# The low parts of the up-projection's weights: a subtraction on VectorE, or a negated copy and a DMA that adds

## The chip, the cores and the metric

The kernel runs on one core of one Trainium2 chip. The metric is the device time of one execution in microseconds. The profiled execution and the three timed runs are executions of the same program. PE is TensorE, DVE is VectorE, ACT is ScalarE, POOL is GpSimd, SP is the engine that only issues DMAs here.

## The reference

One decoder layer over 1024 tokens of width 1024, in float32. The part that the change touches is the gated MLP:

```python
def conv_ffn(xn, w_up, conv_w, conv_b, w_down):      # w_up: 1024 x 5632
    u = xn @ w_up
    upad = jnp.pad(u, ((0, 0), (CONV_WIDTH - 1, 0), (0, 0)))
    c = conv_b
    for j in range(CONV_WIDTH):
        c = c + upad[:, j:j + S] * conv_w[j]
    gate, val = jnp.split(c, 2, axis=-1)
    return (jax.nn.silu(gate) * val) @ w_down
```

Ahead of it stand an RMSNorm, two attention branches, their merge and a mixing projection; behind it a last RMSNorm.

## The kernel before, in words

Every float32 matrix product is made of three products of a reduced type, fp32r: an operand is split into a high part (a cast on ACT) and a low part (operand minus high part, on DVE), and PE adds high by high, high by low and low by high into one PSUM bank. The stages follow each other: input projection (`project`), attention, branch merge (`rest`), mixing projection (`mix`), up-projection (`hidden`), down-projection (`down`).

The change lies in `hidden`, which the profile shows from about 680 us to about 1100 us. The weights come as 22 pairs of 128 columns, one for the gate (`g`) and one for the value (`v`). A pair and the two halves of the tokens make a 2x2 block product, done with seven products in place of eight. The weight operands of the seven are `A11` and `A12` (the two halves of `g`), four sums `S1` to `S4`, and `A22` (half of `v`). So for each pair:

- SP loads `g` into a `raw` tile (three buffers) and `v` into an `rv` tile (two buffers).
- POOL makes the sums: `sa` (S1, S2) and `sb` (S3, S4), two instructions of 128x512 each, into `sf` tiles (two buffers: one for `sa`, one for `sb`, each used again by the next pair).
- `split_pair` splits four tiles: `g` into `wh`, `wl`; `sa` into `sh`, `sl`; `sb` into `sh`, `sl` (three buffers of each for both); half of `v` into another `wh`, `wl` (one buffer). These are the lines L127 (cast on ACT) and L128 (subtraction on DVE).
- PE multiplies in the order P1 (A11), P2 (A12), P5 (S1), P6 (S2), P7 (S3), P3 (S4), P4 (A22), 12 matmuls each, 84 for a pair.
- DVE and one ACT copy put the seven results together into two `us` tiles (`recombine`, L461 to L470); POOL multiplies each by the norm's factors (L1083); ACT and DVE do the convolution, the silu and the gating in `glu_halves` (L1089 to L1094); SP stores the result to `hd`.

The weights of pair j+1 are taken, and those of pair j+2 begun, while PE works on pair j. Each engine runs its own queue in order, and an instruction that waits holds back all behind it on its engine. A scheduler sets the order in the queues when the program is built; `issue_after` and `high_priority` steer it. A tile's buffer is written again only when all that read it are done. Below, pair A is the one that PE works on, B the next, and "C" the one after B.

Of the kernel before, what the change touches and what calls it, by code (L numbers as in the profile page):

```python
# [10 lines left out]
F32 = mybir.dt.float32  # L11
F32R = mybir.dt.float32r
AF = mybir.ActivationFunctionType
ALU = mybir.AluOpType
# [10 lines left out]
NF = DFF // P  # L25
# [19 lines left out]
class Trunk:  # L45
    def __init__(self, tc, ins, out):
        self.tc, self.nc = tc, tc.nc
        (self.xT, self.w_in, self.w_br, self.w_mix, self.w_up, self.w_dn,
         self.vecs_d, self.bias_d) = ins
        self.out = out  # L50
        self.uid = 0
        self.stores = []
        self.uw = self.w22 = self.behind = None
        self.pin, self.after = False, None
        self.hs, self.defer, self.late = {}, [], []

    def name(self, s):
# [12 lines left out]
    def ahead(self, n):  # L70
        while len(self.wq) < n and self.wsrc and (self.wsrc[0][1] != "pair" or self.uw):
            src, nk, *eng = self.wsrc.pop(0)
            if nk == "sums":

                self.sums = self.split_pair(*self.sum_pair(src, True, "sl"), 1, 3)
            elif nk == "rest":
                self.sums["A22"] = self.load_w(src[1][:, 4:8], 4)
                self.wq.append(self.sums)
            elif nk == "second":
                self.wq.append(self.second_pair(src, *eng))  # L80
            elif nk == "idle":
                self.wq.append(self.load_w(src, 8, None, (self.uw, "sh", "sl")))
            elif nk == "pair":
                first, skip = eng or (False, 0)
                self.wq.append(self.split_pair(*self.sum_pair(src, first), skip))
            else:
                self.wq.append(self.load_w(src, nk, *eng))
        if self.deep and self.wsrc and len(self.wsrc[0]) == 2 and not isinstance(self.wsrc[0][1], str):

            src, nk = self.wsrc[0]  # L90
            self.wsrc[0] = src, nk, None, None, self.load_raw(src, nk)
# [20 lines left out]
    def split_pair(self, g, v, sa, sb, skip=0, end=4):  # L112

        nc = self.nc
        ops = {}
        for pool, h, l, src, names in ((self.wp, "wh", "wl", g, ("A11", "A12")), (self.uw, "sh", "sl", sa, ("S1", "S2")),
                                       (self.uw, "sh", "sl", sb, ("S3", "S4")), (self.w22 or self.wp, "wh", "wl", v[:, 1:2], ("A22",)))[skip:end]:
            n = len(names)
            hi = self.tl(pool, [P, n, 4, P], h, F32R)
            lo = self.tl(pool, [P, n, 4, P], l, F32R)  # L120
            with ExitStack() as queue:
                if self.pin and ops:
                    for i in done:
                        queue.enter_context(self.tc.issue_after(i.ins))
                if self.after is not None and names[0] == "A11":
                    queue.enter_context(self.tc.issue_after(self.after.ins))
                i = nc.scalar.copy(hi, src)  # L127
                j = nc.vector.tensor_tensor(lo, src, hi.bitcast(F32), ALU.subtract)  # L128
            if not ops:
                done = i, j  # L130
            if names[0] in ("A11", "A22"):
                ops["made", names[0]] = i, j
            for i, name in enumerate(names):
                ops[name] = hi[:, i], lo[:, i]
        self.pin, self.after = False, None
        return ops
# [1310 lines left out]
```

## Time and profile before

| | us |
|---|---|
| median of 3 runs | 1343.81 (1343.46 to 1343.99) |
| the profiled execution | 1342.57 |
| its span, first to last instruction | 1340.4 |
| PE busy in the span | 1319.8 (98%) |
| DVE busy | 1068.0 (80%) |
| ACT busy | 621.2 (46%) |
| POOL busy | 497.0 (37%) |
| subtractions on L128, all stages | 87.6 + 76.6 + 49.3 in three groups |

The granted TensorE clock of the core is 0.997. POOL issues no DMA at all in this kernel: the queues with dynamic DMAs are those of SP and ACT. The busy share of an engine is an average over stages with different limits, so the stage of the up-projection is read by itself below, in stretches and in single instructions in order of time.

### The profile page before, as it was taken

To read this page: it belongs to the slowest core of one execution; us is meant where nothing else is said; L and a number is where in the kernel's file an instruction comes from. 1 tells how busy PE (TensorE), PEld (TensorE's weight loads), DVE (VectorE), ACT (ScalarE), POOL (GpSimd) and SP (SyncE) were. 2 spreads that over 40 slices of the span, in tenths; PEclk is the share of its full clock that TensorE was granted. 3 is DMA by queue.
4 is the path that set the end of the run, shared out by engine and by line. 5 is a ranking of instruction groups with operands and counts; after the bars stand their busy time and mean duration, and the time that the engine had idled before them with its cause. 6 is when DMAs were issued, how large, how long until landed. Compare 5 with 4: busy or idle time off the path is not lost.

```text
span 1340.4 us, 17301 instructions
## 1 busy us (share of the span) xinstructions
PE 1319.8 (98%) x6264; PEld 1096.7 (82%) x6264; DVE 1068.0 (80%) x1605; ACT 621.2 (46%) x1019; POOL 497.0 (37%) x365
## 2 busy tenths in 40 slices
PE   7999999999999999999999999999999999999997
PEld 6888888888888778878888888888888888888787
DVE  8847775289889876565678999999999997979975
ACT  8432232276667665333454444444444444323544
POOL 0436552000102124651446555655556510224412
PEclk9999999999999999999999999999999999999999
DMA  6423343876553235334423122222222239672333
GB/s 258 151 103 150 147 157 141 247 181 189 142 139 132 91 120 196 141 111 157 133 104 110 64 95 79 94 79 79 95 79 90 75 97 336 203 259 63 114 123 126
DMA packets 63045, 182.64 MB, mean 136 GB/s; under 512 B 6896, under 2 KB 15216, under 8 KB 62960
## 3 DMA queue, kind: packets, MB, share of 16 engines
q1 hardware_dynamic: 51504, 164.13, 37.3%
q10 hardware_dynamic: 11456, 17.41, 3.6%
q8 instruction: 49, 0.80, 0.2%
q14 instruction: 36, 0.29, 0.1%
HBM read 130.66 MB, written 50.86 MB: 135 GB/s over the span
## 4 chain that ended last, share of the span: by engine, by line
PE 87%; DVE 4%; POOL 4%; DMA 2%; ACT 1%; issue 1%; POOLq 0%; SPq 0%; ACTq 0%; DVEq 0%
PE t L922 13%; PE t L920 13%; PE t L921 13%; PE g L209 3%; PE t L914 3%; PE g L210 3%; PE g L211 3%; PE sc L636 3%; PE y L1159 2%; PE d L1159 2%; PE sc L211 2%; PE d L921 2%; PE d L920 2%; PE sc L209 2%; PE sc L210 2%; PE d L922 2%
## 5 line engine op out<-in xcount | busy, mean ns | idle before, releaser
L1089 ACT ACTIVATE c<-us,vecs 128x512 f32<-128x512 f32 x80 | 61.3, 781 | 133.2 <-POOL us L1083 129.2
L1091 DVE SCALAR_TENSOR_TENSOR c<-us,vecs,c 128x512 f32<-128x512 f32 x160 | 110.5, 748 | 8.6 <-ACT c L1089 8.5
L1083 POOL TENSOR_TENSOR us<-us,rstd 128x1024 f32<-128x1024 f32 x38 | 99.7, 2642 | 4.5 <-DVE us L469 2.5
L128 DVE TENSOR_TENSOR sl<-sf,sh 128x1024 fp32r<-128x1024 f32 x62 | 87.6, 1415 | 11.5 <-ACT sh L127 11.5
L127 ACT CAST sh<-sf 128x1024 fp32r<-128x1024 f32 x62 | 63.4, 1048 | 60.3 <-PE t L921 43.9
L176 DVE TENSOR_TENSOR wl<-raw,wh 128x1024 fp32r<-128x1024 f32 (+2 forms) x46 | 57.7, 1256 | 31.4 <-ACT wh L174 20.0
L128 DVE TENSOR_TENSOR wl<-raw,wh 128x1024 fp32r<-128x1024 f32 (+1 forms) x35 | 76.6, 2187 | 3.7 <-ACT wh L127 3.6
L103 POOL TENSOR_TENSOR sf<-rv 128x512 f32<-128x512 f32 x30 | 41.2, 1375 | 100.9 <-DVE sl L128 57.9
L174 ACT CAST wh<-raw 128x1024 fp32r<-128x1024 f32 (+2 forms) x46 | 46.0, 1001 | 62.6 <-PE sc L210 30.5
L209 PE MATMUL g<-xh,wh 128*128 128x512 f32 x176 | 70.6, 401 | 0.1
L211 PE MATMUL g<-xh,wl 128*128 128x512 f32 x176 | 70.4, 400 | 0.0
L210 PE MATMUL g<-xl,wh 128*128 128x512 f32 x176 | 70.3, 399 | 0.0
L108 POOL TENSOR_TENSOR sf<-raw,rv 128x512 f32<-128x512 f32 x30 | 40.7, 1357 | 65.4 <-DVE sl L128 65.4
L619 POOL MEMSET aT<- 128x128 f32 x32 | 6.1, 204 | 151.6 <-PE t L665 101.3
L640 DVE CUSTOM_DVE_ANT_0 L<-sc,bias 128x128 f32<-128x128 f32 (+7 forms) x64 | 47.7, 752 | 17.0 <-PE sc L636 13.7
L641 ACT ACTIVATE L<-L,sm 128x128 f32<-128x128 f32 (+7 forms) x64 | 49.6, 779 | 20.0 <-DVE sm L640 17.4
L794 POOL TENSOR_TENSOR gr<-gr,rstd 128x1024 f32<-128x1024 f32 x16 | 39.9, 2500 | 41.6 <-DMA gr<-gd 41.5
L128 DVE TENSOR_TENSOR wl<-rv,wh 128x512 fp32r<-128x512 f32 x30 | 49.3, 1644 | 3.5 <-ACT wh L127 3.5
L1093 ACT ACTIVATE c<-c 128x512 f32<-128x512 f32 x40 | 23.9, 598 | 60.7 <-DVE c L1091 60.7
L636 PE MATMUL sc<-u,u 128*128 128x512 f32 (+2 forms) x192 | 49.7, 358 | 0.0
L211 PE MATMUL sc<-mh,wl 128*128 128x512 f32 x126 | 49.1, 390 | 0.4 <-DVE wl L176 0.4
L229 POOL TENSOR_TENSOR rs<-ms,mhalf 128x8 f32<-128x8 f32 (+2 forms) x9 | 13.6, 1516 | 95.7 <-DVE ms L227 85.1
(527 smaller groups left out, 4432.7 us busy)
## 6 DMA issues: line engine op xcount, KB each, us to landing
u<-qd SPq DMA_DIRECT2D x72, 256.0 KB, 6.4
raw<-in_w_in SPq DMA_DIRECT2D x25, 512.0 KB, 4.2
raw<-in_w_up SPq DMA_DIRECT2D x23, 512.0 KB, 3.5
hr<-hd SPq DMA_DIRECT2D x46, 256.0 KB, 5.3
hd<-c SPq DMA_DIRECT2D x22, 512.0 KB, 2.6
rv<-in_w_up SPq DMA_DIRECT2D x21, 512.0 KB, 3.5
raw<-in_w_down SPq DMA_DIRECT2D x19, 512.0 KB, 4.3
gr<-gd SPq DMA_DIRECT2D x16, 512.0 KB, 3.6
```

What stands on the lines that cost most here:

```text
L127: i = nc.scalar.copy(hi, src)
L128: j = nc.vector.tensor_tensor(lo, src, hi.bitcast(F32), ALU.subtract)
L209: nc.tensor.matmul(ps, wh[:, kc + o, :], ah, start=first and n == 0, stop=False)
L210: nc.tensor.matmul(ps, wh[:, kc + o, :], al, start=False, stop=False)
L211: nc.tensor.matmul(ps, wl[:, kc + o, :], ah, start=False, stop=last and n == len(kcs) - 1)
L636: nc.tensor.matmul(sc[:, lo + n0:lo + n1], qs, k[c][part][:, n0:n1], start=part == 0, stop=part == 1)
L920: nc.tensor.matmul(ps, ah[:, k, :], bh, start=first and n == 0, stop=False, skip_group_check=skip)
L921: nc.tensor.matmul(ps, ah[:, k, :], bl, start=False, stop=False, skip_group_check=skip)
L922: i = nc.tensor.matmul(ps, al[:, k, :], bh, start=False, stop=last and n == len(ks) - 1, skip_group_check=skip)
L1083: (nc.vector if j == 0 else nc.gpsimd).tensor_tensor(u[:, 2:], u[:, 2:], self.rstd, ALU.mult)
L1089: nc.scalar.activation(c, u[:, o + 2:o + 2 + H2], AF.Identity, bias=self.vecs[:, C_CB + m:C_CB + m + 1], scale=col(m, 2))
L1091: nc.vector.scalar_tensor_tensor(c, u[:, o + k:o + k + H2], col(m, k), c, ALU.mult, ALU.add)
```

## The change

From the third pair of the up-projection on, the low part is made in another way. ACT writes the negated high part into the low tile (one more ACT instruction for each split), and POOL issues a DMA that adds the raw operand, read from SBUF, onto it. The flag `by_dma` is set when a pair is begun and counts pairs (nine pairs belong to the input projection; the first pair of the up-projection is begun elsewhere and isn't counted). It is true for the third to the last pair of the up-projection, and it is still true when the first sums of the down-projection are split (`"sums"`, two tiles). In all there are 82 such DMAs: 62 of 128x1024 (512 KB each) and 20 of 128x512 (256 KB each). The high parts, the products and their order on PE stay.

```diff
         self.pin, self.after = False, None
+        self.by_dma, self.npairs = False, 0
...
                 first, skip = eng or (False, 0)
+                self.npairs += 1
+                self.by_dma = len(self.pairs) + 1 < self.npairs < len(self.pairs) + NF
                 self.wq.append(self.split_pair(*self.sum_pair(src, first), skip))
...
                 i = nc.scalar.copy(hi, src)
-                j = nc.vector.tensor_tensor(lo, src, hi.bitcast(F32), ALU.subtract)
+                if self.by_dma:
+                    j = nc.scalar.mul(lo, hi.bitcast(F32), -1.0)
+                    nc.gpsimd.dma_start(lo, src, accum_op=ALU.add)
+                else:
+                    j = nc.vector.tensor_tensor(lo, src, hi.bitcast(F32), ALU.subtract)
```

In the program the changed lines stand seven lines further down (L127 is L130, L103 is L106, L1083 is L1090). A semaphore named DMASW counts DMAs that POOL issued, DMAHW those of SP and ACT.

POOL's queue before, one pair in the middle of the stage (`us` 7265 and 7266 are the results of the pair before the one on PE, `sf` 7436 and 7437 are `sa` and `sb` of a pair to come):

```order
L1083 TENSOR_TENSOR us_7265<-us_7265,rstd 128x1024 [waits DVE_49]
L1083 TENSOR_TENSOR us_7266<-us_7266,rstd 128x1024 [waits DVE_49]
L103 TENSOR_TENSOR sf_7436<-rv_7434 128x512 [waits DMAHW2_49,Activation_49,Pool_49]
L107 TENSOR_TENSOR sf_7436<-sf_7436,raw_7432 128x512 [waits DMAHW5_49,Pool_49]
L1082 MEMSET us_7421 128x2 [waits DVE_49,Activation_49]
L108 TENSOR_TENSOR sf_7437<-raw_7432,rv_7434 128x512 [waits DVE_49]
L109 TENSOR_TENSOR sf_7437<-raw_7432,sf_7436 128x512 [waits Pool_49]
```

POOL's queue now, one pair in the middle of the stage. `sl_7318` is the low part of S3, S4 of pair A (read by P7), `wl_7323` that of A22 of pair A (read by P4), `sf_7461` is `sb` of pair B, `sl_7472` the low part of S1, S2 of B, `us` 7444 and 7445 are the results of the pair ahead of A, and `sf_7619`, `rv_7617`, `wl_7626` and `raw_7615` belong to pair C:

```order
L133 DMA sl_7318<-sf_7302 128x1024 [waits Activation_49]
L1089 MEMSET us_7603 128x2 [waits DVE_49]
L111 TENSOR_TENSOR sf_7461<-raw_7456,rv_7458 128x512 [waits DMASW7_49]
L112 TENSOR_TENSOR sf_7461<-raw_7456,sf_7460 128x512 [waits Pool_49]
L1090 TENSOR_TENSOR us_7444<-us_7444,rstd 128x1024 [waits DVE_49]
L133 DMA sl_7472<-sf_7460 128x1024 [waits Activation_49]
L1090 TENSOR_TENSOR us_7445<-us_7445,rstd 128x1024 [waits DVE_49]
L133 DMA wl_7323<-rv_7299 128x512 [waits DMASW5_49,Activation_49]
L106 TENSOR_TENSOR sf_7619<-rv_7617 128x512 [waits DMAHW6_49,DMASW0_49,Pool_49]
L1089 MEMSET us_7604 128x2 [waits DVE_49,Activation_49,Pool_49]
L133 DMA wl_7626<-raw_7615 128x1024 [waits DMAHW7_49,DMASW2_49,Activation_49]
L110 TENSOR_TENSOR sf_7619<-sf_7619,raw_7615 128x512 [waits Pool_49]
```

Behind these twelve rows the next `sl` DMA begins the same sequence for the next pair. Four DMA issues stand between POOL's eight instructions of a pair, and where the sums waited for DVE they wait for POOL's own DMAs (DMASW7 is the DMA that wrote `sl_7318`, DMASW0 the one that wrote `sl_7472`).

SP's queue before, in the middle of the stage (`rv` is the load of a `v`, `hd` the store of a result):

```order
L98 DMA raw_7742<-in_w_up 128x1024 [waits DMAHW3_49,DVE_49,Pool_49]
L1095 DMA hd<-c_7307 128x1024 [waits DVE_49]
L100 DMA rv_7589<-in_w_up 128x1024 [waits DMAHW7_49,DMAHW5_49,DVE_49]
L98 DMA raw_7897<-in_w_up 128x1024 [waits DMAHW6_49,DVE_49,Pool_49]
L1095 DMA hd<-c_7462 128x1024 [waits DVE_49]
```

SP's queue now, with the load of `rv_7617` for pair C:

```order
L101 DMA raw_7774<-in_w_up 128x1024 [waits DMASW2_49,Activation_49,Pool_49]
L103 DMA rv_7458<-in_w_up 128x1024 [waits DMAHW3_49,DMAHW5_49,DMASW5_49,Activation_49]
L1102 DMA hd<-c_7331 128x1024 [waits DMAHW4_49,DVE_49]
L101 DMA raw_7933<-in_w_up 128x1024 [waits DMASW6_49,Activation_49,Pool_49]
L103 DMA rv_7617<-in_w_up 128x1024 [waits DMAHW0_49,DMAHW6_49,DMASW1_49,Activation_49]
```

The order of the three kinds of DMA is the same; the loads of `raw` and `rv` wait for POOL's DMAs (DMASW1 is the one that wrote `wl_7323`) where they waited for DVE.

## The prediction

> **What bounds the kernel now.** I read the page's busy times first, then stretches of the up-projection by themselves, then single instructions of each engine in order of time. The page:
>
> ```profile
> span 1340.4 us, 17301 instructions
> PE 1319.8 (98%) x6264; PEld 1096.7 (82%) x6264; DVE 1068.0 (80%) x1605; ACT 621.2 (46%) x1019; POOL 497.0 (37%) x365
> ```
>
> PE is idle for 1340.4 - 1319.8 = 20.6 us in the whole span, and that is all that any relief of another engine could give back. Where it lies shows in the busy times by stretch (length, then PE, PEld, DVE, ACT, POOL, granted clock, DMA share, GB/s):
>
> ```profile
> 740.00:1050.00 310.00, 310.00 (x1370) 256.68 (x1369) 301.09 (x352) 133.45 (x182) 173.90 (x133) 1.00 0.25 83
> 1090.00:1190.00 100.00, 100.00 (x442) 82.80 (x442) 80.79 (x105) 39.69 (x58) 15.60 (x11) 1.00 0.68 229
> 1190.00:1340.00 150.00, 140.44 (x677) 117.59 (x675) 118.63 (x161) 61.39 (x96) 49.98 (x32) 0.97 0.37 130
> ```
>
> In the steady part of the up-projection PE is busy 310.00 of 310.00 us. DVE is at 301.09 of 310 (97%), but PE never waits for it. So the stage is PE's, and its length is the number of pairs by the time of 84 matmuls. PE's own timeline gives that time, the first matmul of pairs 3, 9, 10 and 22 (j = 2, 8, 9 and 21 in the code):
>
> ```profile
> 723.09 0.39 PE L914 MATMUL t<-B_0h,wh 128*128 128x512 f32 x1
> ...
> 837.33 0.39 PE L914 MATMUL t<-B_0h,wh 128*128 128x512 f32 x1
> 856.37 0.39 PE L914 MATMUL t<-B_0h,wh 128*128 128x512 f32 x1
> ...
> 1084.85 0.39 PE L914 MATMUL t<-B_0h,wh 128*128 128x512 f32 x1
> ```
>
> The period T is 856.37 - 837.33 = 19.04 us, and (1084.85 - 723.09) / 19 = 19.04 as well: no pair is late. A product takes 19.04 / 7 = 2.72 us, so with s the start of a pair P7 starts at s + 10.9 and P4 at s + 16.3; its first use of a low part is the third matmul, so A22's low part is due at s + 16.8.
>
> What the other engines do in a pair is in the groups of the stretch 740 to 1050 (busy us, mean ns | idle before, what ended it):
>
> ```profile
> L1083 POOL TENSOR_TENSOR us<-us,rstd 128x1024 f32<-128x1024 f32 x33 | 88.0, 2685 | 4.4 <-DVE us L469 2.5
> L128 DVE TENSOR_TENSOR wl<-raw,wh 128x1024 fp32r<-128x1024 f32 x16 | 47.7, 2981 | 0.0
> L128 DVE TENSOR_TENSOR sl<-sf,sh 128x1024 fp32r<-128x1024 f32 x34 | 43.2, 1269 | 0.0
> L127 ACT CAST sh<-sf 128x1024 fp32r<-128x1024 f32 x33 | 33.0, 1046 | 0.1
> L128 DVE TENSOR_TENSOR wl<-rv,wh 128x512 fp32r<-128x512 f32 x17 | 31.0, 1822 | 0.0
> L108 POOL TENSOR_TENSOR sf<-raw,rv 128x512 f32<-128x512 f32 x17 | 22.0, 1295 | 53.0 <-DVE sl L128 53.0
> L103 POOL TENSOR_TENSOR sf<-rv 128x512 f32<-128x512 f32 x16 | 20.7, 1293 | 29.3 <-DMA rv<-in_w_up 28.0 <-DVE sl L128 1.3
> L127 ACT CAST wh<-rv 128x512 fp32r<-128x512 f32 x17 | 10.6, 621 | 7.0 <-PE t L921 7.0
> ```
>
> POOL already waits twice in each pair for a buffer that the splits hold: about 53.0 / 17 = 3.1 us until DVE has read `sb`, and 28.0 / 16 = 1.8 us until the next `v` has been loaded. Both waits lie in the chain that the change lengthens.
>
> **What is removed.** For each of 20 pairs DVE loses 2.98 + 2 x 1.27 + 1.82 = 7.3 us, and two more subtractions of 1.27 us in the down-projection's first sums: about 149 us. PE waited for none of it in this stage, so it is worth nothing directly. It does free POOL: the group above has 2.69 us for a multiplication by `rstd`, but the spread within it is wide.
>
> ```profile
> L1083 POOL TENSOR_TENSOR us<-us,rstd x38: 1992/2448/2982, 733.8 to 1070.0; 128x1024 f32<-128x1024 f32 x38
> L128 DVE TENSOR_TENSOR wl<-raw,wh x35: 686/2432/3024, 59.1 to 1217.8; 128x1024 fp32r<-128x1024 f32 x31, 128x512 fp32r<-128x512 f32 x4
> ```
>
> (least, median, longest ns.) With DVE's subtractions gone I take the least, 1.99 us; with the mean the sum below would have 1.4 us more a pair. The Trainium skill (SBUF — State Buffer, Who interferes with whom) says that a DVE instruction with both inputs in SBUF contends with a GpSimd instruction that reads SBUF. By that rule the 1.99 us should be reached, since no such DVE instruction is left in a pair; without it the total below would be some 25 us higher.
>
> **What is added on ACT and the DMA engines.** The negations are 62 of 128x1024 and 20 of 128x512. At the casts' price that is 62 x 1.046 + 20 x 0.621 = 77 us, 3.8 us a pair. ACT goes from 133.45 / 310 x 19.04 = 8.2 us to 12.0 us of 19.04: covered. The DMAs write 3 x 512 + 256 KB = 1.84 MB a pair, 96 GB/s beside the 83 GB/s at which the engines are 0.25 busy; even counted twice that leaves room. Nothing queued on SP behind the load of `rv` is wanted earlier: it is the store of a result that ACT and DVE finish after that.
>
> **What is added on POOL, the term that decides.** POOL now issues four DMAs a pair, and two instructions wait for one of these to land. I follow POOL's queue as shown above from the `sl` DMA of S3, S4 of one pair to that of the next:
>
> 1. the `sl` DMA is issued and must land (call it X512), as the next `sb` overwrites what it reads;
> 2. two sums, 2 x 1.29;
> 3. the first `rstd` multiplication, 1.99; a DMA issue (q); the second, 1.99;
> 4. the `wl` DMA of A22 is issued and must land (X256), since it reads the `rv` buffer that pair C's `v` is to be loaded into;
> 5. SP loads that `v`, and POOL makes the first sum from it;
> 6. a sum 1.29, a DMA issue (q), a sum 1.29; then step 1 again.
>
> Step 5 is seen in the timelines of DVE, SP and POOL today, where DVE's subtraction stands in the place of the DMA:
>
> ```profile
> 862.23 1.89 DVE L128 TENSOR_TENSOR wl<-rv,wh 128x512 fp32r<-128x512 f32 x1
> 864.15 0.33 SPq L100 DMA_DIRECT2D rv<-in_w_up  x1
> 867.74 1.29 POOL L103 TENSOR_TENSOR sf<-rv 128x512 f32<-128x512 f32 x1 [1.76 <-DMA rv<-in_w_up]
> ```
>
> From the buffer's release (862.23 + 1.89 = 864.12) to POOL's sum it is 3.6 us. So a turn takes C = 2.58 + 3.98 + 3.6 + 2.58 + 2q + X512 + X256 = 12.74 + 2q + X512 + X256. No row has a DMA issued by POOL, nor one that adds, so q and X are bounded by the nearest rows: DMA issues (KB each, median us to landing), and the smallest arithmetic on POOL.
>
> ```profile
> u<-qd SPq DMA_DIRECT2D x72, 256.0 KB, 6.4
> hd<-c SPq DMA_DIRECT2D x22, 512.0 KB, 2.6
> rv<-in_w_up SPq DMA_DIRECT2D x21, 512.0 KB, 3.5
> xr<-in_xT SPq DMA_DIRECT2D x7, 512.0 KB, 7.2
> gd<-u ACTq DMA_DIRECT2D x2, 256.0 KB, 2.8
> out_T<-x ACTq DMA_DIRECT2D x2, 256.0 KB, 2.1
> L229 POOL TENSOR_TENSOR rs<-ms,mhalf 128x8 f32<-128x8 f32 (+2 forms) x9 | 13.6, 1516 | 95.7 <-DVE ms L227 85.1
> ```
>
> For q: not under SP's 0.33 us, hardly over the 1.5 us of POOL's smallest operation; I take 0.9, the middle. For the landing: the two transfers of this very stage take 2.6 and 3.5 us for 512 KB, mean 3.05; 256 KB take 2.1 to 2.8, mean 2.45. An addition moves three streams (two read, one written) where a copy moves two, so I take 1.5 times: X512 = 0.9 + 4.6 = 5.5 and X256 = 0.9 + 3.7 = 4.6. Then C = 12.74 + 1.8 + 10.1 = 24.6 us, 5.6 us over T. Low ends: q 0.33 and copies of 2.6 and 2.1 us issue included, C = 18.1. High ends: q 1.5, 7.2 and 6.4, C = 29.3.
>
> **The sum.** Pair 3 (s = 723.09) is the first. A22's one buffer is free when P4 of pair 2 has ended, 723.5; cast and negation bring 724.7. One X256 and one turn later A22 of pair 4 has landed: 724.7 + 4.6 + 24.6 = 753.9. It is due at 723.09 + 19.04 + 16.8 = 758.9, so 5.0 us are in hand. 18 turns follow up to pair 22, each 5.6 us longer than PE's: 18 x 5.6 - 5.0 = 96 us. The two DMAs in the down-projection are far from use. The profiled execution had 1342.57 us, so 1439; from the median of 1343.81, about **1440 us**.
>
> **The rivals.** I count 0.2% (2.7 us) as what a measurement can tell from no change.
>
> *Hidden* (0.10): the turn fits under PE's. That needs 18 (C - 19.04) to stay below 758.9 - 724.7 - X256 - C, which with X256 = 3 means C under 19.7. At the low ends C is 18.1 and PE waits nowhere: 1344 us, not slower. For it: POOL is busy only 173.90 of 310 us in the stage, and `hd<-c` does leave SBUF in 2.6 us. Against it: q would have to be near SP's 0.33 us and the addition as quick as the quickest copy.
>
> *Cheap additions* (0.20): an addition costs a copy's time behind the issue, X512 = 0.9 + 2.6 and X256 = 0.9 + 2.1. C = 12.74 + 1.8 + 6.5 = 21.0; 18 x 2.0 less 10.2 in hand (34.2 - 3.0 - 21.0) is 26 us, so 1370. For it: most of these 2 to 3 us doesn't grow with the size (2.1 for 256 KB, 2.6 for 512), so a third stream may cost little. The Trainium skill (DMA: Bandwidth & Descriptors, Anatomy of one DMA — SWDGE (gpsimd) path) has about 2.0 us plus bytes over 436 GB/s for a DMA on this path, and about 1 us to its first byte. An estimate from that page is 3.2 and 2.6 us with q = 1, so C = 20.5 and 1360 us; no run here shows yet that it holds for a DMA that adds.
>
> *Dear additions* (0.18): the adding itself is slow, or POOL is held for longer than 1.5 us by an issue. At the high ends C = 29.3; 18 x 10.3 + 1.6 is 187 us, so 1531, and more if an addition takes over 7 us. For it: DMAs of 256 KB do take 6.4 us where the queues are full, and POOL's small operations show a start cost of 1.5 us. Against it: the DMA engines are a quarter busy in this stage.
>
> *Faster* (0.02): PE's 20.6 us of idling would have to shrink, and almost none of it lies behind the stage's splits (9.6 us are in the last 150 us).
>
> **How the numbers follow.** The forecast, C from 22.3 to 27.5, has 0.50; it spans 1395 to 1495. The range 1362 to 1545 leaves out the hidden case, the cheapest additions and the dearest, about 2 in 10. Faster 0.02, the same 0.10, slower 0.88.
>
> **What would show it.** Right: in the steady stretch PE idles some 5 to 6 us a pair ahead of P4's first low matmul, released by the `wl<-rv` DMA; POOL idles ahead of the `sb` sum (on the `sl` DMA, about 4.6 us) and ahead of the first sum (on `rv`, about 8 us); pair starts are 24 to 25 us apart; the landings are 5.5 and 4.6 us; `rstd` multiplications take 2.0 us. Wrong: PE stays at 310 of 310 (hidden); pair starts under 22 us apart (cheap); PE released by ACT or DVE, or DMA engines busy throughout (another bound); POOL issues that each hold it for several us.

## The result and the profile after

The changed kernel takes 1431.43 us (median of 6 runs, 1427.77 to 1434.04); the kernel before took 1342.67 us in the same comparison (6 runs). The ratio is 1.066 [1.0647, 1.0673], so the change costs 6.6%. The profiled execution has a span of 1432.0 us, 91.6 us more than before.

The page of the kernel after, its span and the busy times:

```profile
span 1432.0 us, 17503 instructions
PE 1358.6 (95%) x6264; PEld 1111.6 (78%) x6264; DVE 936.9 (65%) x1523; ACT 696.9 (49%) x1101; POOL 541.1 (38%) x447
```

DVE loses 131 us and POOL, for all its new work, is busy 38% of the time. No engine's share betrays a bound. The same stretch of the up-projection as before, by engines (length, then PE, PEld, DVE, ACT, POOL, granted clock, DMA share, GB/s):

```profile
740.00:1050.00 310.00, 276.44 (x1112) 217.71 (x1112) 152.91 (x226) 156.34 (x201) 164.11 (x157) 0.94 0.60 147
```

PE, which had no idle time here, has 33.6 us of it, and it does less in the stretch: 1112 recorded matmuls where there were 1370. The pair starts in PE's timeline (j = 4, 10 and 21):

```profile
768.74 0.40 PE L921 MATMUL t<-B_0h,wh 128*128 128x512 f32 x1
...
908.39 0.39 PE L921 MATMUL t<-B_0h,wh 128*128 128x512 f32 x1
...
1168.38 0.39 PE L921 MATMUL t<-B_0h,wh 128*128 128x512 f32 x1
```

The mean period is (1168.38 - 768.74) / 17 = 23.5 us, 4.5 over T; single pairs take 20.1 to 26.8 us. Pair 22 starts 83.5 us later than before (1168.38 against 1084.85), so all but 8 us of the 91.6 lie ahead of that start, in this loop. Of the 8, 4.9 are one wait of PE ahead of the down-projection's first matmul, for DVE's last result of pair 22 (`d L1166 <- DVE us L477`). POOL's timeline shows one turn of the loop, with SP's load in its place:

```profile
886.81 1.19 POOL L133 DMA_DIRECT2D sl<-sf  x1
...
893.79 1.29 POOL L111 TENSOR_TENSOR sf<-raw,rv 128x512 f32<-128x512 f32 x1 [5.67 <-DMA sl<-sf]
895.04 1.29 POOL L112 TENSOR_TENSOR sf<-raw,sf 128x512 f32<-128x512 f32 x1
896.28 1.99 POOL L1090 TENSOR_TENSOR us<-us,rstd 128x1024 f32<-128x1024 f32 x1
898.22 0.87 POOL L133 DMA_DIRECT2D sl<-sf  x1
898.84 2.29 POOL L1090 TENSOR_TENSOR us<-us,rstd 128x1024 f32<-128x1024 f32 x1
900.79 1.21 POOL L133 DMA_DIRECT2D wl<-rv  x1
907.94 1.29 POOL L106 TENSOR_TENSOR sf<-rv 128x512 f32<-128x512 f32 x1 [5.95 <-ACT c L1100]
...
909.23 0.87 POOL L133 DMA_DIRECT2D wl<-raw  x1
909.83 1.58 POOL L110 TENSOR_TENSOR sf<-sf,raw 128x512 f32<-128x512 f32 x1
911.07 1.18 POOL L133 DMA_DIRECT2D sl<-sf  x1
```

```profile
904.43 0.33 SPq L103 DMA_DIRECT2D rv<-in_w_up  x1
```

This is the turn that the prediction followed row by row: 911.07 - 886.81 = 24.3 us here, one of the longer ones (from 793 us on they take 23.2 to 24.8). POOL stands still twice, ahead of the `sb` sum until the `sl` DMA has landed, and ahead of the first sum until A22's DMA has landed and `v` has been loaded. The bracket at 907.94 names `ACT c L1100`, but that instruction is no input of the sum; SP's load, issued 3.5 us earlier, is. POOL's waits from 760 to 1160 us (us in total, times, longest) and the landings (KB, median us from issue):

```profile
POOL sf L111 <- DMA sl<-sf: 84.1, 17, 6.2
POOL sf L106 <- ACT c L1100: 78.4, 13, 6.1
POOL sf L106 <- DMA rv<-in_w_up: 18.4, 4, 6.0
```

```profile
sl<-sf POOLq DMA_DIRECT2D x40, 512.0 KB, 5.1
wl<-raw POOLq DMA_DIRECT2D x20, 512.0 KB, 5.2
wl<-rv POOLq DMA_DIRECT2D x20, 256.0 KB, 3.5
```

PE's timeline around P4 shows what it waits for:

```profile
902.51 0.50 PE L927 MATMUL t<-T_0h,wh 128*128 128x512 f32 x1 [1.97 <-ACT s L468]
...
904.41 0.51 PE L929 MATMUL t<-T_0h,wl 128*128 128x512 f32 x1 [1.16 <-DMA wl<-rv]
904.74 0.60 PE L927 MATMUL t<-T_1h,wh 128*128 128x512 f32 x1
905.15 0.63 PE L928 MATMUL t<-T_1l,wh 128*128 128x512 f32 x1
```

It waits 1.16 us for A22's low part, at the place that was forecast, but 1.97 us just before that for an ACT copy that frees a PSUM bank. ACT's timeline says why that copy is late:

```profile
898.31 0.78 ACT L1096 ACTIVATE c<-us,vecs 128x512 f32<-128x512 f32 x1 [7.81 <-POOL us L1090]
901.16 0.78 ACT L1096 ACTIVATE c<-us,vecs 128x512 f32<-128x512 f32 x1 [2.07 <-POOL us L1090]
901.88 0.58 ACT L468 COPY s<-t 128x512 f32<-128x512 f32 x1
```

It stands in ACT's queue behind the convolution of the pair before, which waits for POOL's `rstd` multiplications; these come after the first landing. So both of PE's waits come from the late POOL. After them the matmuls run 0.43 us apart until the next pair starts at 908.39, where 0.227 is the rule.

### The profile page after: what moved, and what is told of

It reads as the page before. It is cut to its first block, busy times and chain, and to the rows that moved or that the text cites. A ratio compares the mean times of both kernels' runs of the same rounds, so it can differ in the third digit from the quotient of the medians.

```text
span 1432.0 us, 17503 instructions
## 1 busy us (share of the span) xinstructions
PE 1358.6 (95%) x6264; PEld 1111.6 (78%) x6264; DVE 936.9 (65%) x1523; ACT 696.9 (49%) x1101; POOL 541.1 (38%) x447
## 5 line engine op out<-in xcount | busy, mean ns | idle before, releaser
L1098 DVE SCALAR_TENSOR_TENSOR c<-us,vecs,c 128x512 f32<-128x512 f32 x160 | 115.3, 752 | 214.0 <-ACT c L1096 212.4
L130 ACT CAST sh<-sf 128x1024 fp32r<-128x1024 f32 x62 | 64.8, 1047 | 90.4 <-PE t L928 43.6
L106 POOL TENSOR_TENSOR sf<-rv 128x512 f32<-128x512 f32 x30 | 41.9, 1395 | 176.4 <-ACT c L1100 78.4
L1090 POOL TENSOR_TENSOR us<-us,rstd 128x1024 f32<-128x1024 f32 x38 | 81.5, 2162 | 0.0
L236 POOL TENSOR_TENSOR rs<-ms,mhalf 128x8 f32<-128x8 f32 (+2 forms) x9 | 13.7, 1520 | 95.3 <-DVE ms L234 84.7
L216 PE MATMUL sc<-mh,wh 128*128 128x512 f32 x126 | 49.0, 389 | 0.0
L217 PE MATMUL sc<-ml,wh 128*128 128x512 f32 x126 | 49.0, 389 | 0.0
L110 POOL TENSOR_TENSOR sf<-sf,raw 128x512 f32<-128x512 f32 x31 | 48.0, 1549 | 0.9
L882 POOL TENSOR_TENSOR rstd<-rstd,t 128x512 f32<-128x512 f32 x14 | 21.9, 1577 | 68.7 <-ACT t L881 68.7
```

Of the source, the lines that this page charges most:

```text
L110: tt(sa[:, 1], sa[:, 0], g[:, 0], ALU.subtract)
L216: nc.tensor.matmul(ps, wh[:, kc + o, :], ah, start=first and n == 0, stop=False)
L217: nc.tensor.matmul(ps, wh[:, kc + o, :], al, start=False, stop=False)
L1090: (nc.vector if j == 0 else nc.gpsimd).tensor_tensor(u[:, 2:], u[:, 2:], self.rstd, ALU.mult)
L1098: nc.vector.scalar_tensor_tensor(c, u[:, o + k:o + k + H2], col(m, k), c, ALU.mult, ALU.add)
```

## The experiments

Two explanations were to be told apart. **The queue:** each DMA, negation and sum is cheap enough, but POOL waits in its own queue for DMAs that it issued itself, and these waits close a loop. **The price:** 82 adding DMAs and 82 negations cost time by themselves (DMA engines, POOL's issue time, ACT, a lower clock).

### The same DMAs in another order

All 82 DMAs and negations stay. The `rstd` multiplications are put into POOL's queue ahead of the next pair's DMAs, and the `sb` sums behind them:

```diff
+                if 0 < j < NF - 2:
+                    self.scale(j, us)
                 if j < NF - 1:
...
                     w, ps = ready[j + 1] = self.next_w(), {}
...
-        tt(sb[:, 0], g[:, 0], v[:, 0], ALU.subtract)
-        tt(sb[:, 1], g[:, 1], sa[:, 1], ALU.subtract)
+        with self.tc.issue_after(self.scaled.ins) if self.by_dma and self.scaled is not None else nullcontext():
+            tt(sb[:, 0], g[:, 0], v[:, 0], ALU.subtract)
+            tt(sb[:, 1], g[:, 1], sa[:, 1], ALU.subtract)
...
```

(`scale` holds the memset and the `rstd` multiplication of each result, which stood in `glu_halves`.)

> All 82 DMAs stay; only the place of POOL's two rstd multiplications of a pair and of the A22 DMA moves: now they stand between the sl DMA of S3, S4 and the sb sums that wait for its landing. If the loss is POOL's closed turn (two landings waited out one after the other), the turn becomes 0.6 + 3.9 + 0.6 us up to the A22 DMA, then 3.6 + 3.5 us to the next v and about 2.5 us of sums, some 15 us, under PE's 19.04: pair starts 19.0 us apart and about 1344 us (1340 to 1352). If the loss is the price of the DMAs themselves (adding, DMA engines, POOL's issue time) or of ACT's negations, the same work is still there: 1420 to 1435.

Measured: 1342.76 us, ratio 0.9996 [0.9986, 1.0006]. The whole loss is gone with every DMA still there. The stretch of the up-projection, and POOL's queue in it:

```profile
740.00:1050.00 310.00, 310.00 (x1370) 256.68 (x1369) 193.11 (x283) 197.20 (x248) 211.56 (x201) 1.00 0.74 183
```

```profile
890.74 0.85 POOL L134 DMA_DIRECT2D sl<-sf  x1
...
893.64 1.99 POOL L1091 TENSOR_TENSOR us<-us,rstd 128x1024 f32<-128x1024 f32 x1 [1.93 <-DVE us L477]
895.59 0.86 POOL L134 DMA_DIRECT2D sl<-sf  x1
896.37 2.12 POOL L1091 TENSOR_TENSOR us<-us,rstd 128x1024 f32<-128x1024 f32 x1
898.32 1.02 POOL L134 DMA_DIRECT2D wl<-rv  x1
898.92 1.75 POOL L112 TENSOR_TENSOR sf<-raw,rv 128x512 f32<-128x512 f32 x1
```

The landing of the `sl` DMA (890.74) is now spent on the multiplications, and the `sb` sum (898.92) waits for nothing. PE is at 310.00 of 310 again, with the DMA engines at 0.74, more than in any other of these kernels. The price, taken as a whole, is nothing. The new order opens every loop that runs through this landing, so this run alone does not say which of them set the pace.

### One part of the DMAs at a time

The line `if self.by_dma:` in `split_pair` is narrowed to one or two of the four tiles, or to all but one; the others keep DVE's subtraction:

```diff
-                if self.by_dma:
+                if self.by_dma and names[0] in ("A11", "S1"):    # A11 and A12, S1 and S2
+                if self.by_dma and names[0] in ("S3", "A22"):
+                if self.by_dma and names[0] in ("S3",):          # S3 and S4 alone
+                if self.by_dma and names[0] in ("A22",):
+                if self.by_dma and names[0] != "S3":             # all but S3 and S4
+                if self.by_dma and names[0] != "A22":
```

(one of these lines in each kernel.) A11, A12 and S1, S2, whose landing was expected to hold back nothing on the turn:

> Only the low parts of A11, A12 and of S1, S2 go by negation and DMA (1 MB a pair, 41 DMAs); S3, S4 and A22 by DVE as before. Closed turn: sb waits for DVE and the next v for DVE, the one landing waited for (S1, S2 ahead of the next sa) is half covered by an rstd multiplication; the turn is under 19 us: 1344 (1340 to 1352). A price per DMA or per byte: half or more of the 89 us, 1385 to 1395.

S3, S4 and A22, the two landings of the turn:

> Only the low parts of S3, S4 and of A22 go by negation and DMA (0.75 MB a pair, 41 DMAs); A11, A12 and S1, S2 by DVE. Both landings are still waited out one after the other on POOL: about 5.0 + 2.5 + 3.9 to 4.9 + 3.6 + 3.5 + 2.5 = 21 to 22 us a turn, 2 to 3 us over PE's, less some 10 us in hand at the start: 1368 to 1386. A price per byte would give 43% of the loss, 1381, so this run tells only together with e2.

Measured: 1344.39 us (1.0008 [0.9994, 1.0022]) for the first (called e2 in the expectations), 1375.73 us (1.024 [1.0219, 1.026]) for the second. Both came as the queue has it: 1 MB a pair by 41 DMAs costs nothing, 0.75 MB by 41 others costs 32 us. In the second the `sl` DMA has no neighbour and lands in 4.5 us (median; 5.1 is the median of both `sl` DMAs of the full change); POOL's turn is 20.9 us (`sl` DMA to `sl` DMA, 866.95 to 887.89).

Then each landing of the turn alone. By the prediction's loop neither should be enough:

> Only the low part of S3, S4 goes by negation and DMA (512 KB a pair, 21 DMAs); A22's is back on DVE, so only one landing is waited out on POOL. Closed turn: 4.9 + 2.5 + 4.0 us, the next v (loaded once DVE has read the last) and 2.5 us of sums, 14 to 18 us, under 19.04: 1344 (1340 to 1352). If each DMA or each wait costs by itself, a quarter to a half of the change's 89 us: 1365 to 1388.

> Only the low part of A22 goes by negation and DMA (256 KB a pair, 20 DMAs); sb waits for DVE as before. Closed turn: 3.6 + 3.5 us to the next v, 5.0 us of sums, 4 to 5 us of rstd multiplications, 16 to 18 us, under 19.04: 1344 (1340 to 1352). If each DMA or each wait costs by itself, a quarter to a half of the 89 us: 1365 to 1388.

Measured: A22 alone 1348.79 us (1.0039 [1.0014, 1.0063]), within its range; PE is at 309.81 of 310, and the 6 us lie at the end of the stage. S3, S4 alone (e5) 1390.32 us (1.0352 [1.0322, 1.0382]): **a miss**, and a larger loss than with A22 added to it. In its timelines, POOL first and ACT below it:

```profile
896.35 0.89 POOL L133 DMA_DIRECT2D sl<-sf  x1 [2.84 <-ACT sl L132]
...
900.83 2.04 POOL L111 TENSOR_TENSOR sf<-raw,rv 128x512 f32<-128x512 f32 x1 [3.47 <-DMA sl<-sf]
...
904.08 1.99 POOL L1090 TENSOR_TENSOR us<-us,rstd 128x1024 f32<-128x1024 f32 x1
```

```profile
893.32 0.60 ACT L1100 ACTIVATE c<-c 128x512 f32<-128x512 f32 x1 [1.48 <-DVE c L1098]
893.81 1.04 ACT L130 CAST sh<-sf 128x1024 fp32r<-128x1024 f32 x1
894.88 1.06 ACT L132 ACTIVATE sl<-sh 128x1024 fp32r<-128x1024 f32 x1
```

There is a second loop, through ACT. The DMA for S3, S4 waits for ACT's negation (`<-ACT sl L132`). The cast and the negation stand in ACT's queue behind the silu of the pair before; the silu waits for DVE's convolution taps, these for ACT's copy of `c`, that for POOL's `rstd` multiplications, which stand behind the `sb` sums, which wait for the landing of the last `sl` DMA. From the first multiplication of one pair (882.66) to that of the next (904.08) it is 21.4 us, 2.4 over T. Pair 22 starts 43.8 us later than before (1128.68 against 1084.85), and 47.6 us were lost in all.

With A22 added, the run before this one, ACT's queue has another order: from its first copy of `c` to the end of that negation it takes 10.3 us (897.35 to 907.70) where here it takes 11.2 (884.70 to 895.94). Its loop is about 19.8 us there, so POOL's own loop of 20.9 sets the pace, and the kernel with more DMAs is the faster one. This is read from the traces; no run tests it.

This reading was tested by shortening the loop where POOL and the DMAs have no part in it: in the same kernel the two convolution taps on DVE are left out (a part of the result is missing; only the time is read).

```diff
-                for k in (1, 0):
-                    nc.vector.scalar_tensor_tensor(c, u[:, o + k:o + k + H2], col(m, k), c, ALU.mult, ALU.add)
```

> Only S3 and S4 by adding DMAs, as in e5, and the two convolution taps per half that VectorE adds between ScalarE's copy of c and its silu left out (part of the result is left out; only the time is read). If e5 was held by a second turn through ScalarE's queue (landing, two sums, two rstd multiplications, copy of c, taps, silu, cast and negation of S3 and S4: 21.4 us of a period of 19.04), this turn loses about 5 us and falls under the period: 1344, range 1336 to 1356. If the adding DMA itself or POOL's own queue cost e5 its 48 us, nothing of that has changed: about 1385 to 1395.

> The full change with the same two taps left out. If POOL's own turn (two landings, the sums and the multiplications; no convolution in it) sets the pace by itself, the time stays near the full change's: 1415 to 1435. If the turn through ScalarE alone set it, it would fall by some 3 us or more a pair to 1344 to 1385. In between, both are needed.

Measured: with S3, S4 alone and no taps 1344.26 us (1.0014 [1.0003, 1.0025]): the 48 us are gone, so the second loop, through the convolution, is shown. The full change without taps: 1396.01 us (1.0397 [1.0367, 1.0427]), between the two expectations, and not a clean test: the `wl` DMA of A11, A12 has moved in POOL's queue ahead of the first sum. POOL's timeline of it:

```profile
896.46 0.86 POOL L133 DMA_DIRECT2D wl<-raw  x1 [3.43 <-ACT wl L132]
897.24 1.41 POOL L106 TENSOR_TENSOR sf<-rv 128x512 f32<-128x512 f32 x1
...
899.96 0.86 POOL L133 DMA_DIRECT2D sl<-sf  x1
...
904.43 1.28 POOL L111 TENSOR_TENSOR sf<-raw,rv 128x512 f32<-128x512 f32 x1 [3.50 <-DMA sl<-sf]
```

The `sl` DMA follows the other 512 KB by 3.5 us and the sum can start 4.5 us after its issue; in the full change it follows by 1.8 us, and it is 6.0 to 7.5 us, mostly 6.1. The turn is 21.4 us here (`sl` DMA to `sl` DMA, 899.96 to 921.40), so most of what was saved is that landing.

Last, the full change less one of the two landings of the turn:

> The full change, but S3 and S4 keep DVE's subtraction: 62 of the 82 adding DMAs stay (A11 and A12, S1 and S2, A22). Both turns pass through the landing of the DMA for S3 and S4; without it neither is closed: 1344 to 1352 (the 6 us that A22 alone lost at the end of the stage may stay). If each landing cost its own time, with A22's 3.5 us still in POOL's queue each pair, the loss would be more than a third of the full change's: over 1370.

> The full change, but A22 keeps DVE's subtraction: 62 adding DMAs stay. The turn through POOL and the load of rv is shorter by A22's landing (about 20 us left, near PE's 19.04); the turn through ACT stays, and in the full change it measures about 22.3 us: 20 x (21.4 to 23.0 less 19.04) above before, so 1390 to 1425. If POOL's turn with both landings were the only one that counts: 1344 to 1365.

Measured: without S3, S4's DMAs 1343.98 us (1.0012 [0.9999, 1.0026]), although 61 of the 82 DMAs are still there and A22's still stands in POOL's queue. Without A22's 1399.08 us (1.0424 [1.039, 1.0457]), inside its range. The pair starts of the latter (durations, first and last start):

```profile
L921 PE MATMUL t<-B_0h,wh x7: 389/499/504, 828.1 to 962.0; 128*128 128x512 f32 x7
```

(962.0 - 828.1) / 6 = 22.3 us a pair (22.0 from 740.96 to 1136.5), the length forecast for the loop through ACT. Here POOL's `sl` DMA waits for ACT's negation; in the full change that negation has ended 1.1 us before POOL issues the DMA at 911.07:

```profile
897.63 0.87 POOL L133 DMA_DIRECT2D sl<-sf  x1 [1.45 <-ACT sl L132]
```

```profile
908.93 1.06 ACT L132 ACTIVATE sl<-sh 128x1024 fp32r<-128x1024 f32 x1
```

(the kernel without A22's DMAs first, the full change below it). So the loops are nested, and both run through the landing for S3, S4. Through ACT alone it is 57 us, and A22's landing, which makes POOL's own loop the longer one, adds the other 32 of the 89.

### The sizes: an adding DMA, more work on PE, the negations

The DMA copies where it added (the low parts are then the raw operand; only the time is read):

```diff
-                    nc.gpsimd.dma_start(lo, src, accum_op=ALU.add)
+                    nc.gpsimd.dma_start(lo, src)
```

> The changed kernel with the addition taken out of the DMA: it copies the raw operand over the low part, so the low parts are wrong, and only the time is read. If an addition costs 1.5 times a copy, as the prediction took it, the landings fall by a third behind the issue (512 KB from about 5.1 to 3.9 us, 256 KB from 3.5 to 2.7), a turn by some 2.5 us, and the time to about 1385. If an addition costs what a copy costs, nothing changes: 1425 to 1437.

Measured: 1370.63 us (1.0206 [1.0176, 1.0235]). Its landings:

```profile
sl<-sf POOLq DMA_DIRECT2D x40, 512.0 KB, 3.4
wl<-raw POOLq DMA_DIRECT2D x20, 512.0 KB, 2.9
wl<-rv POOLq DMA_DIRECT2D x20, 256.0 KB, 2.3
```

An addition takes 5.1 / 3.4, 5.2 / 2.9 and 3.5 / 2.3 of that, 1.5 to 1.8 times as long. The time fell further than expected for a factor of 1.5.

P3 computed twice in 18 pairs, 12 more matmuls each (2.72 us):

```diff
+                if name == "P3" and 2 < j < NF - 1:
+                    self.product(ps[name], w[a], b)
```

> The changed kernel with P3 of 18 pairs computed twice into the same bank (12 more matmuls a pair, 2.72 us at full clock; the result is the same). If POOL's turn is the bound and PE only waits, the matmuls fill PE's wait: 1431 to 1440. If PE is the bound (its lower granted clock behind the waits, or its own queue), 18 x 2.72 = 49 us more: about 1480.

Measured: 1438.21 us (1.0705 [1.0683, 1.0726]). PE gets 18 x 2.72 = 49 us more work and the kernel takes 7 us longer, so PE isn't the bound in the loop. Its clock there is 0.99 where the full change has 0.94: the low clock follows from the waits and doesn't make them.

ACT's negations kept, DVE adding instead of the DMA:

```diff
-                    nc.gpsimd.dma_start(lo, src, accum_op=ALU.add)
+                    j = nc.vector.tensor_tensor(lo, src, lo.bitcast(F32), ALU.add)
```

> ACT's 82 negations stay, and DVE adds the raw operand onto them in place of the DMA. If the loss is POOL's closed turn, it is gone, and the negations (3.8 us a pair on an ACT that is busy for 8.2 of 19.04) cost nothing: 1344 (1340 to 1352). If the negations hold up ACT's queue, it stays well above: over 1360.

Measured: 1356.99 us (1.0104 [1.0043, 1.0164]), between the two expectations. PE's busy time, 308.24 of 310 in the steady stretch, hides a part of the loss: from 819.44 to 1092.45 us the pair starts are 19.5 us apart, 0.46 over T, which makes 6.5 us in 14 pairs. The rest lies at the end of the stage (PE is busy 36.33 of 40 us from 1090 to 1130). The traces show the loop through ACT here too, with DVE's addition in the place of the landing: POOL's first `rstd` multiplications start at 866.07, 885.58 and 905.09, 19.51 us apart; ACT's copy of `c` waits for them, the negation stands behind taps and silu, DVE's addition waits for the negation (0.64 us), and POOL's `sb` sum for the addition (3.78 us). The negations are free in the reordered kernel, so they aren't dear as such. That this loop is the cause is read from the trace and not tested, and the loss at the end of the stage stays open. This kernel also shows POOL's multiplication. The group from 740 to 1050 us here, and in the full change:

```profile
L1090 POOL TENSOR_TENSOR us<-us,rstd 128x1024 f32<-128x1024 f32 x32 | 92.1, 2898 | 3.7 <-DVE us L477 1.7
```

```profile
L1090 POOL TENSOR_TENSOR us<-us,rstd 128x1024 f32<-128x1024 f32 x26 | 55.5, 2134 | 0.0
```

2.90 us with DVE adding from two SBUF tiles, 2.13 without, 2.69 before.

## Why the prediction was right, and where its steps were off

**The time and the mechanism held.** 1440 was forecast, 1431 measured. The stage turned from PE's to POOL's, and the queue's two waits are where they were put: 84.1 / 17 = 4.9 us and (78.4 + 18.4) / 17 = 5.7 us a turn, where 4.6 and 8 were forecast. The reordering shows that the cost lies in the order of the queues and not in the DMAs, and the run without S3, S4's DMAs that it hangs on their landing.

**The terms of the turn were off in both directions.** The landing for S3, S4, X512, was put at 5.5 us; issue to sum is 6.0 to 7.5 from 793 us on, mostly 6.1 (6.98 in the rows above), with the 512 KB for A11, A12 issued 1.8 us earlier. Without that neighbour it is mostly 4.5. The prediction priced each DMA by itself, and this is the term that came out too small. A22's landing, X256, was put at 4.6 and is 3.5. An issue, q, was put at 0.9; the next instruction on POOL starts 0.6 us after it (898.22 to 898.84). Its upper bound, the 1.5 us of POOL's smallest operation, was a mean of unlike forms, with single instructions of 0.7 to 2.6 us. The step from `rv`'s release to the sum was 3.6 and is 3.5. In sum 23.5 us where 24.6 was forecast, and the errors cancel for the most part. 17 pairs at 4.5 over T, one of 6.5 (743.16 to 768.74) and the 8 us behind the start of pair 22 make nearly all of the 91.6 us. The prediction's sum had 96 us in the turns, where 83.5 were measured, and nothing for those 8 us, so part of the closeness of 1440 to 1431 is luck.

**The factor for adding was an assumption, and it holds:** 1.5 was taken and 1.5 to 1.8 measured. The rival with cheap additions fell on this. The Trainium skill (DMA: Bandwidth & Descriptors, Anatomy of one DMA — SWDGE (gpsimd) path) gave an estimate of 3.2 and 2.6 us; the copies here land near it (2.9 to 3.4, and 2.3), the additions don't (5.1 and 3.5), so its figure isn't one for a DMA that adds.

**The multiplication at its least value held,** 1.99 us for the first of each pair, 2.13 in the mean. The rule of the Trainium skill (SBUF — State Buffer, Who interferes with whom) agrees with the measurement in both directions: 2.13 without DVE instructions that read two SBUF inputs, 2.90 with such additions put back. What counts is the overlap: with only S3, S4 and A22 by DMA, DVE still subtracts (889.84 and 891.57, 1.22 us each), but not beside the multiplications (895.33 to 899.28), and these take 1.99 us.

**The step that failed is "covered" for ACT.** ACT is busy half the time, 156.34 of 310 us, and its casts and negations still come late, since what counts is the place in its queue: behind the convolution that waits for POOL. That gave a second loop, 22.3 us (with A22 left on DVE) against POOL's 23.5. The prediction didn't have it, and had only A22 been left on DVE, its reasoning would have forecast nearly no loss where 57 us was measured. The forecast of the full change was right because the loop that it did see is the longer one.

**Where PE waits was half right.** It waits at P4, but of its 33.6 us of idling from 740 to 1050 only 13.7 (in 13 waits) are for A22's low part; 19.4 (in 11) come just before, for the PSUM bank that ACT frees late. Together that is 2.5 us a pair where 5 to 6 were forecast; the rest of the 4.5 is matmuls further apart behind the waits (276.44 / 1112 = 0.249 us each, before 310.00 / 1370 = 0.226).

## What to carry to other kernels

When work moves from an engine with slack to a DMA, look at who must wait for its landing before the next issue: an in-order queue that issues a DMA, and a few instructions later needs a buffer that this DMA reads, is a closed loop with the landing in it, and its length counts against the period, not the engine's busy share. Follow such a loop through every in-order queue that it touches, ACT's too, and look for the cure in the order: independent work put between issue and wait made 89 us vanish here without one DMA less. No version tried beats the kernel before, for PE is busy without a gap in this stage and an idle DVE is worth nothing to it.

## What the runs showed of the hardware

Short waits cost PE more than their length. By stretches of the full change (the columns as above), the waits of 1.97 and 1.16 us with the matmuls behind them, and the start of the next pair:

```profile
902.00:909.00 7.00, 5.32 (x15) 3.94 (x16) 6.74 (x10) 5.97 (x9) 1.06 (x1) 0.76 0.42 114
909.00:924.00 15.00, 15.00 (x68) 12.41 (x67) 4.76 (x8) 5.02 (x6) 10.19 (x11) 1.00 0.63 156
```

The granted clock is 0.76 in the first and 1.00 in the second, and the matmuls are 0.43 us apart for 3.7 us. The Trainium skill (TensorE: Matmul & The Clock Gate, Part 1: The HAM clock gate) has half the rate after an idle window of about 3.4 us; here two waits of 3.1 us together, with matmuls between them, were enough. In the kernel with one wait of about 1 us a pair (S3, S4 and A22 by DMA) the clock stays at 1.00. Since POOL sets the pace, the slow matmuls cost no time here.

An adding DMA close behind another on POOL's queue lands later: from the issue of 512 KB to the sum that waits for them it took mostly 4.5 us alone (up to 6.2) or 3.5 us behind another 512 KB (4.4 to 5.0), and 6.0 to 7.5 us when 1.8 us behind it.
